# Latent layers: second attention's projections and rotation ahead of the gated linear attention's levels, one projection for two sets of values; context gates applied behind PSUM; key copies issued by GpSimd

## The chip, the cores and the metric

The kernel runs on one core of a Trainium2 chip. The metric is device time in microseconds (us) of one execution. The engines are named PE (TensorE, matmuls), DVE (VectorE), ACT (ScalarE), POOL (GpSimd) and SP (SyncE, which issues most of the DMAs); each has an instruction queue of its own, executed in order.

## The reference, cut to what matters

Two blocks are computed one after the other, in float32. The first (dilated attention with an mLSTM, cross attention, a mixture of 16 experts) is not touched. The second has two layers, in which a latent stream `x` (512 tokens, width 1024) and a context stream `ctx` (256 tokens) go through three mixers side by side: a neighbourhood attention (na, 6 heads of 64), a gated linear attention (GLA, 4 heads) and a grouped-query attention (GQA, 6 query and 2 key heads). The latent stream's two attentions also read the context's keys and values. One input projection feeds all three:

```python
(na_q, na_k, na_v, gl_q, gl_k, gl_v, gl_g, gl_lr, ga_q, ga_k, ga_v) = jnp.split(u @ w_in, IN_SPLITS, axis=-1)
# widths 384, 384, 384, 128, 128, 256, 256, 32, 384, 128, 128
...
o = jnp.concatenate([merge_heads(o_na), gla_output(o_gl, gla_norm_w, gl_g), merge_heads(o_ga)], axis=-1)
...
x = layer_norm(DEEPNORM_ALPHA * x + g1 * (o @ w_out[l]), ln1_g[l], ln1_b[l])
x = layer_norm(DEEPNORM_ALPHA * x + g2 * swiglu(modulate(x, sh2, sc2), w_ffn_in[l], w_ffn_out[l]), ln2_g[l], ln2_b[l])
if ctx_out:     # layer 0 only
    xc = layer_norm(DEEPNORM_ALPHA * xc + g1c * (oc @ w_out[l]), ln1_g[l], ln1_b[l])
    xc = layer_norm(DEEPNORM_ALPHA * xc + g2c * swiglu(modulate(xc, sh2c, sc2c), w_ffn_in[l], w_ffn_out[l]), ln2_g[l], ln2_b[l])
```

GQA's queries and keys are normed by head (rms) and rotated by an axial position table ahead of the scores. The gates g1, g2 (g1c, g2c) are one row of 1024 numbers for all tokens.

## The kernel before

**Products.** Every float32 operand is split into a high part (`w_h`, a cast by ACT, L350) and a low part (`w_l`, the rest, a subtraction by DVE, L351), and a product is three matmuls, high by high, high by low and low by high (L343). A weight chunk goes DMA (`raw`, L380) → optionally a multiplication by a row on POOL (L387) → the two splits → matmuls. A projection by tokens (`proj_tok`, matmuls named `pj`) goes over column blocks of up to 512, each into one PSUM bank per tile of 128 tokens (four for the latent stream, two for the context); with K = 1024 that is 8 × 3 × 4 = 96 matmuls per column block of the latent stream and 48 of the context. A projection by features (`pf`) takes 128 columns at a time.

**Order.** The framework orders each engine's instructions when the kernel is built: by the place in the program among those that its own timeline takes to be ready. So of two pieces of work that are both ready, the one written earlier goes first, and later work fills the gaps. Buffers and PSUM banks are given out in that order. Several places write the order out by hand, with Python generators that are advanced piece by piece.

**Stages.** Until about 480 us the first block runs up to its experts. From there to 1204 us the experts run in the background of the context stream's layer 0 (its second stream of weight chunks), to 1284 us the context's layer 1 (keys and values only). Then come latent layer 0 (1284 to 1978 us) and latent layer 1 (to the end).

**A layer** (`layer2`, L2149) runs `gla` first: the gate inputs (L1839), the gates themselves (L1848 to L1862), q and k, a projection of 512 columns for v and the output gate, transposed decayed keys (`gltp`, L1906), the chunk states (`gls`), eight levels `lv` that fill the attention matrix (L1943 to L2002: on POOL a difference `glD`, on ACT two exponentials for each direction and scaled copies `glqb`, on DVE products `glxk` and `glxq`, on PE the matmuls `glG`), and the output products (`glo`, L2013 and L2017). `finish` norms, gates and transposes its output (`otp`, L2035). Then `gqa` (L1700): a projection of 512 columns for q and k (L1719), one of 128 for v (L1721), through `between` the neighbourhood attention's 384 columns for its values (`na_v`, L1575), then for each tile of tokens the rotation on DVE and POOL, a transposition (`gtp`, L1783) and the splits. Between these, `woven` advances `na_kq` (L1585), which projects the neighbourhood attention's first pair of keys (K0) and queries (Q0) and later those of pairs 1 and 2. The scores (`sc`, L542 and L543) of the neighbourhood attention follow, with a bias that POOL loads (`na_bias`, L1621).

**Key copies.** Keys stand in two halves of the partitions; `dup_k` (L530) copies each half to the other with four DMAs from SP's queue, for GQA's keys (`gak`) and for each pair of neighbourhood keys (`nak`).

**Gates.** In the latent stream `out_proj` (L2076) multiplies the product by g1 on DVE (`gps`, L2086). In the context stream (`nt < 4`) the gate is multiplied into the weight chunks instead, by POOL, through `row=`: 8 chunks of `w_out` and 22 of `w_ffn_out`, each 128x1024 (L387). `ffn` (L2096) does that in both streams for g2.

## Time and profile before

| | us |
|---|---|
| median of 3 runs (lowest, highest) | 2701.52 (2699.83, 2702.96) |
| profiled execution: its time | 2709.36 |
| profiled execution: span of its trace | 2707.6 |
| PE busy in the span | 2515.4 |
| DVE, ACT, POOL busy | 1725.2, 1281.9, 418.7 |

The span is what the trace covers; 1.8 us of the profiled execution's time lie around it. Durations in the rows are those of this one execution. Matmuls are pipelined, and the duration of one overlaps the next: the cost of many in a row is the length of their stretch over their count, not the mean of one.

### The profile page before, as it was taken

Reading aid. Unit: us, or ns where it says so; the run is one execution under the profiler, and the core shown is the slowest. Engines: PE = TensorE matmul, PEld = TensorE weight load, DVE = VectorE, ACT = ScalarE, POOL = GpSimd, SP = SyncE. Lnnn points to the kernel's source line nnn. Section 1 sums busy time; section 2 is a strip of 40 time slices with the busy share of each in tenths; the row PEclk is TensorE's granted clock in tenths of the full one; section 3 lists DMA queues with packets and bytes.
Section 4 is the critical chain, followed back from the end, with each engine's and each line's share of the span. In section 5 each row is a group of like instructions: output and inputs, shape, how many; then the busy total and the mean of one; then the engine's idle time right before and its main releaser. Section 6 shows DMA issues by size and latency. Waiting matters only on the chain. (4 is left out here: it accounts for less than half of the span.)

```text
span 2707.6 us, 35926 instructions
## 1 busy us (share of the span) xinstructions
PE 2515.4 (93%) x13176; PEld 1963.8 (73%) x13176; DVE 1725.2 (64%) x3117; ACT 1281.9 (47%) x2389; POOL 418.7 (15%) x304
## 2 busy tenths in 40 slices
PE   8999899798889999988998999999989899999997
PEld 5547575676667888877786588888868666888886
DVE  3346646797687787778786665444567776644446
ACT  4344444576655555556656642222266574422221
POOL 1100000201022121022220023111141200411101
PEclk9999899899999999998999999999989999999999
DMA  7765357588777888767254123333323524233331
GB/s 276 208 203 160 117 192 244 159 268 282 250 241 234 268 276 276 252 222 220 81 156 137 69 87 122 96 94 94 104 86 96 146 82 133 71 101 93 94 93 63
DMA packets 355157, 436.54 MB, mean 161 GB/s; under 512 B 20384, under 2 KB 228128, under 8 KB 354976
## 3 DMA queue, kind: packets, MB, share of 16 engines
q1 hardware_dynamic: 350560, 416.90, 49.1%
q0 software_dynamic: 4416, 17.30, 1.8%
q8 instruction: 105, 1.72, 0.3%
q14 instruction: 76, 0.62, 0.1%
HBM read 387.21 MB, written 38.01 MB: 157 GB/s over the span
## 5 line engine op out<-in xcount | busy, mean ns | idle before, releaser
L351 DVE TENSOR_TENSOR w_l<-raw,w_h 128x1024 fp32r<-128x1024 f32 (+2 forms) x530 | 714.5, 1359 | 465.8 <-ACT w_h L350 456.6
L350 ACT CAST w_h<-raw 128x1024 fp32r<-128x1024 f32 (+2 forms) x530 | 527.5, 1007 | 855.6 <-PE pj L343 272.2
L343 PE MATMUL fab<-hTf_h,w_h 128*128 128x512 f32 (+1 forms) x1104 | 386.2, 351 | 4.1 <-ACT hTf_h L514 3.4
L343 PE MATMUL fab<-hTf_h,w_l 128*128 128x512 f32 (+1 forms) x1104 | 386.7, 351 | 0.5 <-DVE w_l L351 0.4
L343 PE MATMUL fab<-hTf_l,w_h 128*128 128x512 f32 (+1 forms) x1104 | 386.2, 350 | 0.2
L387 POOL TENSOR_TENSOR raw<-raw,g2b 128x1024 f32<-128x1024 f32 x66 | 172.3, 2617 | 708.5 <-DMA raw<-in_w_ffn_out 615.1
L343 PE MATMUL pj<-w_l,hT_h 128*128 128x512 f32 (+3 forms) x608 | 229.8, 379 | 14.1 <-DVE w_l L351 14.1
L343 PE MATMUL pj<-w_h,hT_h 128*128 128x512 f32 (+3 forms) x608 | 222.2, 378 | 14.9 <-ACT w_h L350 9.9
L343 PEld LDWEIGHTS fab<-hTf_h,w_h 128*128 128x128 f32 x1104 | 208.9, 190 | 37.2 <-ACT hTf_h L514 4.5
L343 PEld LDWEIGHTS fab<-hTf_h,w_l 128*128 128x128 f32 x1104 | 209.2, 190 | 32.8 <-DVE w_l L351 1.2
L343 PEld LDWEIGHTS fab<-hTf_l,w_h 128*128 128x128 f32 x1104 | 209.2, 190 | 32.2 <-DVE hTf_l L515 0.6
L343 PE MATMUL pj<-w_h,hT_l 128*128 128x512 f32 (+3 forms) x608 | 225.0, 372 | 0.0
L343 PE MATMUL pj<-w_h,wk_h 128*128 128x512 f32 x376 | 148.5, 401 | 7.9 <-DVE x L2107 4.9
L343 PEld LDWEIGHTS pj<-w_h,hT_h 128*128 128x128 f32 x608 | 118.6, 197 | 45.8 <-ACT w_h L350 13.4
L343 PEld LDWEIGHTS pj<-w_l,hT_h 128*128 128x128 f32 x608 | 120.5, 198 | 42.4 <-DVE w_l L351 18.3
L343 PE MATMUL pj<-w_l,wk_h 128*128 128x512 f32 x376 | 150.0, 400 | 1.1 <-DVE w_l L351 0.9
L343 PE MATMUL pj<-w_h,wk_l 128*128 128x512 f32 x376 | 147.3, 399 | 1.2 <-DVE wk_l L351 1.2
L343 PE MATMUL pf<-hT_h,w_h 128*128 128x512 f32 (+3 forms) x376 | 133.4, 356 | 10.2 <-DVE nak_l L351 3.1
L343 PEld LDWEIGHTS pj<-w_h,hT_l 128*128 128x128 f32 x608 | 120.3, 198 | 22.0 <-issue 5.2
L343 PE MATMUL pf<-hT_h,w_l 128*128 128x512 f32 (+3 forms) x376 | 131.2, 350 | 0.0
L343 PE MATMUL pf<-hT_l,w_h 128*128 128x512 f32 (+3 forms) x376 | 131.2, 350 | 0.0
L577 ACT COPY pT<-ptp 128x512 f32<-128x512 f32 (+3 forms) x184 | 88.5, 497 | 53.5 <-PE ptp L575 52.4
(598 smaller groups left out, 4840.7 us busy)
## 6 DMA issues: line engine op xcount, KB each, us to landing
raw<-in_w SPq DMA_DIRECT2D x192, 512.0 KB
raw<-in_w_ffn_in SPq DMA_DIRECT2D x132, 512.0 KB
raw<-in_w_ada SPq DMA_DIRECT2D x96, 512.0 KB
raw<-in_w_in SPq DMA_DIRECT2D x76, 512.0 KB
raw<-in_w_ffn_out SPq DMA_DIRECT2D x66, 512.0 KB
raw<-in_w_out SPq DMA_DIRECT2D x32, 512.0 KB
yd<-ysb SPq DMA_DIRECT2D x16, 512.0 KB
raw<-in_w_in SPq DMA_DIRECT2D x16, 384.0 KB
```

The source lines that it names most:

```text
L343: self.nc.tensor.matmul(out, lhsT=l, rhs=r, start=first and k == 0 and i == 0, stop=last and k == n - 1 and i == 2, **kw)
L350: nc.scalar.copy(out=hl.hi, in_=src)
L351: nc.vector.tensor_sub(out=hl.lo, in0=src, in1=f32(hl.hi))
L387: self.nc.gpsimd.tensor_tensor(out=raw, in0=raw, in1=row.unsqueeze(1).to_broadcast([P, kt, n]), op=OP.mult)
L577: nc.scalar.copy(out=pT()[:, slice(b0, b0 + bb), ts], in_=tp[:, :bb * P].rearrange("p (b t) -> p b t", t=P))
```

## The change

`w_in`'s columns are put in another order on the host, so that GQA's v (128 columns) and the neighbourhood attention's v (384) are neighbours and one projection of 512 columns makes both, in all four layers (latent and context). `gqa` becomes a generator with two stops: in the latent layers `gla` advances it, once behind its own q and k (GQA's q and k projection), once behind its v and gate projection (the V projection, the rotation, transpositions, splits and key copies), so that all of this stands ahead of GLA's levels in the program. The neighbourhood attention's K0 is started behind `gla`, no longer within the rotation. In the context layers the order stays. In `out_proj` and `ffn` of the context the gate is multiplied by DVE with the product's PSUM tile (`times`), no longer into the weights by POOL. In the latent layers `dup_k` issues from POOL's queue.

```diff
@@ -197,6 +197,9 @@
...
     A["w_out_2"] = np.concatenate([wo[:, :640], wo[:, 640:].reshape(2, 2, 3, 64, D).transpose(0, 2, 1, 3, 4).reshape(2, 384, D)], 1)
+    wi = A["w_in_2"]
+    A["w_in_2"] = np.concatenate([wi[:, :, :768], wi[:, :, 1152:], wi[:, :, 768:1152]], 2)
@@ -520,17 +523,17 @@
...
-    def stack_k(self, k, ps):
+    def stack_k(self, k, ps, eng=None):
...
             self.split(k[r, h], ps[r])
-        self.dup_k(k)
-    def dup_k(self, k):
+        self.dup_k(k, eng)
+    def dup_k(self, k, eng=None):
...
             for h in range(2):
-                self.nc.sync.dma_start(out=f32(t[64 - 64 * h:128 - 64 * h, h]), in_=f32(t[64 * h:64 * h + 64, h]))
+                (eng or self.nc.sync).dma_start(out=f32(t[64 - 64 * h:128 - 64 * h, h]), in_=f32(t[64 * h:64 * h + 64, h]))
@@ -1572,22 +1575,12 @@
...
-    def na_v(self, l, hT, T, W, pool):
-        vd = self.dr.tile([T, 384], F32, name=f"nav{l}{T}")
-        def ev(i, c0, n, ps):
-            v = pool.tile([P, 384], F32, name="nav", tag="nav", bufs=2)
-            self.copy(v, ps[:, :n])
-            self.nc.sync.dma_start(out=vd[i * P:(i + 1) * P, :], in_=v)
-        self.proj_tok(hT, T // P, W[:, 768:1152], ev)
-        return vd
...
         k = g["k"] = self.hl_tile(pool, [P, 2, T], "nak", f"nak{f % 2}")
-        yield from self.feat_pieces(hT, T, W[:, 384 + f * P:384 + (f + 1) * P], lambda ps: self.stack_k(k, ps[:, :T]))
+        yield from self.feat_pieces(hT, T, W[:, 384 + f * P:384 + (f + 1) * P], lambda ps: self.stack_k(k, ps[:, :T], nc.gpsimd if lat else None))
@@ -1697,7 +1690,7 @@
...
-    def gqa(self, l, hT, T, W, ctxd, full, d, keep, pool, between, woven):
+    def gqa(self, l, hT, T, W, ctxd, full, d, keep, pool, got):
@@ -1705,7 +1698,7 @@
...
         nh = nq + 2
-        c0 = 1952 if full else 2336
+        c0 = 1568 if full else 1952
@@ -1717,9 +1710,17 @@
...
         self.proj_tok(hT, nt, W[:, c0:c0 + nh * 64], ev)
+        yield
         v = keep.tile([P, nt, P], F32, name="gav")
-        self.proj_tok(hT, nt, W[:, 2464:2592], lambda i, c0, n, ps: self.copy(v[:, i, :], ps[:, :n]))
-        mid = between()
+        vd = self.dr.tile([T, 384], F32, name=f"nav{l}{T}")
+        def ev_v(i, _, n, ps):
+            self.copy(v[:, i, :], ps[:, :P])
+            t = pool.tile([P, 384], F32, name="nav", tag="nav", bufs=2)
+            self.copy(t, ps[:, P:n])
+            nc.sync.dma_start(out=vd[i * P:(i + 1) * P, :], in_=t)
+        self.proj_tok(hT, nt, W[:, 2080:2592], ev_v)
@@ -1775,8 +1776,6 @@
...
             ff = f.rearrange("p h d -> p (h d)")
-            for _ in range(2):
-                next(woven, None)
@@ -1787,7 +1786,7 @@
...
                 self.split(kS[r2, h, ts], tp[r2, (nb - 1) * P:nb * P])
-        self.dup_k(kS)
+        self.dup_k(kS, nc.gpsimd if lat else None)
@@ -1823,9 +1822,10 @@
...
             return units
-        return attend, mid
-    def gla(self, l, hT, T, W, ctxd, full, d, late, pool):
+        got.extend((attend, vd))
+        yield
+    def gla(self, l, hT, T, W, ctxd, full, d, late, pool, other):
@@ -1836,10 +1836,10 @@
...
         if lat and l:
-            lr_, *qk = self.in_halves(hT, T, [W[:, a:b] for a, b in ((1920, 1952), (1152, 1280), (1280, 1408))], lambda: self.mm("pf"))
+            lr_, *qk = self.in_halves(hT, T, [W[:, a:b] for a, b in ((1536, 1568), (768, 896), (896, 1024))], lambda: self.mm("pf"))
...
         else:
-            self.proj_feat(hT, T, W[:, 1920:1952], lambda f, m, ps: nc.scalar.copy(out=lr, in_=ps[:32, :T]))
+            self.proj_feat(hT, T, W[:, 1536:1568], lambda f, m, ps: nc.scalar.copy(out=lr, in_=ps[:32, :T]))
@@ -1872,7 +1872,8 @@
...
         else:
-            self.proj_feat(hT, T, W[:, 1152:1408] if full else W[:, 1280:1408], ev)
+            self.proj_feat(hT, T, W[:, 768:1024] if full else W[:, 896:1024], ev)
+        next(other, None)
@@ -1886,9 +1887,10 @@
...
                                                op0=OP.mult, op1=OP.mult)
-            self.proj_tok(hT, nt, W[:, 1408:1920], evv)
+            self.proj_tok(hT, nt, W[:, 1024:1536], evv)
         else:
-            self.proj_tok(hT, nt, W[:, 1408:1664], lambda i, c0, n, ps: self.copy(v[:, i, :], ps[:, :n]))
+            self.proj_tok(hT, nt, W[:, 1024:1280], lambda i, c0, n, ps: self.copy(v[:, i, :], ps[:, :n]))
+        next(other, None)
@@ -2065,6 +2067,11 @@
...
+    def times(self, ps, g, pool):
+        t = pool.tile([P, 512], F32, name="gps", tag="gps", bufs=1)
+        self.nc.vector.tensor_tensor(out=t, in0=ps, in1=g, op=OP.mult)
+        return t
@@ -2081,16 +2088,13 @@
...
             s = slice(c0, c0 + n)
-            if nt == 4:
-                t = pool.tile([P, 512], F32, name="gps", tag="gps", bufs=1)
-                nc.vector.tensor_tensor(out=t, in0=ps, in1=g1b[:, s], op=OP.mult)
-                ps = t
-            nc.vector.scalar_tensor_tensor(out=x[:, i, s], in0=x[:, i, s], scalar=ALPHA, in1=ps[:, :n], op0=OP.mult, op1=OP.add)
+            nc.vector.scalar_tensor_tensor(out=x[:, i, s], in0=x[:, i, s], scalar=ALPHA, in1=self.times(ps, g1b[:, s], pool),
+                                           op0=OP.mult, op1=OP.add)
...
         if nt < 4:
-            return self.proj_tok(oT, nt, W, lambda *a: self.call(ev(*a)), row=g1b)
+            return self.proj_tok(oT, nt, W, lambda *a: self.call(ev(*a)))
@@ -2104,6 +2108,8 @@
...
             s = slice(c0, c0 + n)
+            if nt < 4:
+                ps = self.times(ps, g2b[:, s], pool)
@@ -2133,7 +2139,8 @@
...
             if f0 < nf or nt < 4:
-                self.proj_tok(lambda k: gT[:, k, :], nt, rows, ev if f0 < nf else lambda *a: self.call(ev_last(*a)), kt=fg, row=g2b)
+                self.proj_tok(lambda k: gT[:, k, :], nt, rows, ev if f0 < nf else lambda *a: self.call(ev_last(*a)), kt=fg,
+                              row=g2b if nt == 4 else None)
@@ -2159,14 +2166,21 @@
...
             with tpool("gqp") as p2, tpool("gll") as p0:
+                got = []
+                second = self.gqa(l, hT, T, W, ctxd, full, d, keep, p2, got)
                 with tpool("glp") as p1:
-                    finish = self.gla(l, hT, T, W, ctxd, full, d, p0, p1)
+                    finish = self.gla(l, hT, T, W, ctxd, full, d, p0, p1, second if lat else iter(()))
...
                 begun = self.na_kq(0, l, hT, T, W, lat, full, p3, g0, d) if lat else iter(())
-                attend, vd = self.gqa(l, hT, T, W, ctxd, full, d, keep, p2, lambda: self.na_v(l, hT, T, W, p2), begun)
+                if lat:
+                    next(begun)
+                    next(begun)
+                for _ in second:
+                    pass
+                attend, vd = got
```

## Rows read from the trace of the kernel before

**Rows 1.** The page: busy time of the engines, and the chain that ended last.

```profile
PE 2515.4 (93%) x13176; PEld 1963.8 (73%) x13176; DVE 1725.2 (64%) x3117; ACT 1281.9 (47%) x2389; POOL 418.7 (15%) x304
...
PE 19%; DVE 1%; DMA 1%; ACT 0%; issue 0%; DVEq 0%
```

**Rows 2.** Windows: stretch, length, busy (count) per engine, granted PE clock, DMA share, GB/s.

```profile
820.00:1200.00 380.00, 362.32 (x2072) 311.97 (x2072) 293.39 (x308) 210.03 (x261) 66.66 (x29) 0.98 0.78 254
...
1284.00:1400.00 116.00, 116.00 (x788) 97.00 (x787) 86.40 (x168) 72.42 (x152) 27.72 (x30) 1.00 0.38 114
1400.00:1411.00 11.00, 5.50 (x30) 4.79 (x29) 10.69 (x28) 5.22 (x13) 3.14 (x4) 0.69 0.66 213
...
2118.00:2129.00 11.00, 5.37 (x28) 4.51 (x27) 10.65 (x29) 5.04 (x15) 3.14 (x4) 0.84 0.59 191
```

**Rows 3.** Windows of the projections `pj` alone, 512, 128 and 384 columns.

```profile
1294.03:1316.39 22.36, 22.36 (x96) 17.81 (x95) 0.41 (x1) 0.90 (x3) 1.00 0.28 87
1353.52:1355.79 2.27, 2.27 (x19) 2.20 (x19) 0.00 (x0) 0.00 (x0) 1.00 0.23 30
1379.76:1387.93 8.17, 8.17 (x46) 8.01 (x46) 0.00 (x0) 0.96 (x2) 1.00 0.10 33
```

**Rows 4.** Timeline, PE, first latent layer: start, duration, instruction, idle before.

```profile
1316.39 1.04 PE L1906 MATMUL gltp<-cpack,glt 128*128 128x128 f32 x8
...
1329.47 1.08 PE L1981 MATMUL glG<-glqb,glk 128*32 128x128 f32 x32
...
1370.43 0.70 PE L2013 MATMUL glo<-glSc,glqt 128*128 128x256 f32 x2
...
1378.94 1.00 PE L2017 MATMUL glo<-glv,glA 128*128 128x64 f32 x8
...
1406.60 0.58 PE L542 MATMUL sc<-nak_h,naq 128*128 128x256 f32 x1 [3.04 <-DVE glost L351]
```

**Rows 5.** Timeline, DVE, same layer.

```profile
1307.54 0.41 DVE L1962 TENSOR_TENSOR glxk<-glD,glk 128x256 f32<-128x256 f32 x1
...
1308.21 0.68 DVE L1902 TENSOR_TENSOR glt<-glt,glk 128x512 f32<-128x512 f32 x1
```

**Rows 6.** Timeline, ACT, same layer.

```profile
1353.42 0.40 ACT L1960 ACTIVATE glD<-glD 128x256 f32<-128x256 f32 x1
...
1363.22 2.51 ACT L1971 ACTIVATE glqb<-glxq,cpack 128x256 f32<-128x256 f32 x6 [0.51 <-DVE glxq L1963]
```

**Rows 7.** Timeline, SP's queue (SPq: the time an issue held it).

```profile
1419.95 4.27 SPq L533 DMA_DIRECT2D gak_h<-gak_h  x1
...
1427.66 0.94 SPq L533 DMA_DIRECT2D nak_h<-nak_h  x1
```

**Rows 8.** Chain of waits, second latent layer: start, duration, piece.

```profile
2148.92 10.19 DMA nak_l<-nak_l
```

**Rows 9.** The bias tile `nab`, loaded from POOL's queue.

```profile
DMA to landing us min/median/max: 3.8/5.9/8.2
```

**Rows 10.** Groups by line and form, 440 to 1210: busy, mean ns | idle before, releasers.

```profile
L351 DVE TENSOR_TENSOR w_l<-raw,w_h 128x1024 fp32r<-128x1024 f32 x283 | 377.4, 1352 | 126.7 <-ACT w_h L350 122.8 <-PE fab L343 2.7
...
L343 PE MATMUL h<-w_l,ehT_h 128*128 128x512 f32 x256 | 104.2, 407 | 8.5 <-DVE w_l L351 8.5
...
L387 POOL TENSOR_TENSOR raw<-raw,g2b 128x1024 f32<-128x1024 f32 x22 | 58.5, 2664 | 215.7 <-DMA raw<-in_w_ffn_out 156.1 <-DVE w_l L351 37.1 <-DVE wk_l L351 19.7
...
L343 PE MATMUL pj<-w_h,wk_h 128*128 128x512 f32 x88 | 34.8, 420 | 7.9 <-DVE x L2107 4.9 <-ACT w_h L350 2.7 <-ACT wk_h L350 0.2
...
L387 POOL TENSOR_TENSOR raw<-raw,g1b 128x1024 f32<-128x1024 f32 x8 | 20.0, 2509 | 51.8 <-DMA raw<-in_w_out 21.0 <-issue 15.6 <-DMA nak_h<-nak_h 15.2
```

**Rows 11.** Waits of ACT, 440 to 1210: total, times, longest.

```profile
ACT w_h L350 <- POOL raw L387: 53.6, 21, 6.2
```

**Rows 12.** The tile `w_l`, 480 to 1200: ns min/median/max, first and last start.

```profile
L351 DVE TENSOR_TENSOR w_l<-raw,w_h x292: 411/1222/3439, 480.7 to 1198.6; 128x1024 fp32r<-128x1024 f32 x141, 128x256 fp32r<-128x256 f32 x3, 128x768 fp32r<-128x768 f32 x2
```

**Rows 13.** The tile `gps`, whole run.

```profile
L2086 DVE TENSOR_TENSOR gps<-pj,g1b x16: 672/679/693, 1568.2 to 2318.9; 128x512 f32<-128x512 f32 x16
```

## The prediction

> **What bounds the kernel now.** I began with the page's busy shares and its chain of waits. TensorE (PE) is busy in 2515.4 of 2707.6 us, and the chain that ended last runs mostly through PE's matmuls [rows 1]. So a change pays if it takes matmul time away, or one of the stretches in which PE stands still. The table by stretch says where these are [rows 2]. The context layer, with the experts beside it, leaves PE idle for 380.00 − 362.32 = 17.7 us in 820–1200. In the first latent layer's projections (1284–1400) PE is busy for all 116.00 us at a granted clock of 1.00, the upper of its two levels (2.4 GHz). Behind them lies a hole of 11 us with 5.50 us busy, in which the mean granted clock is 0.69, between the upper level and the lower one (1.2 GHz). The second latent layer repeats it at 2118–2129 (5.37 us). So idle time per latent layer is 5.5 us, in which the rotated queries and keys and the first neighbourhood scores are waited for: PE then begins the scores after 3.04 us idle, released by a DVE subtract [rows 4].
>
> **Merged V projection.** It removes 96 matmuls with 128 columns and 96 with 384 in each latent layer and adds 96 with 512. From the three stretches of projection matmuls alone [rows 3], one costs 2.27/19 = 0.1195 us, 8.17/46 = 0.1776 us and 22.36/96 = 0.233 us. Per layer 96 × (0.1195 + 0.1776 − 0.233) = 6.2 us. PE has no idle time there [rows 2], so this is on the path: −12.3 us for both. In each context layer it is 48 × 0.064 = 3.1 us of PE time, but PE there has gaps and experts to fill them; between 0 and −6.2 for both, I take −2.5. Copies out of PSUM move the same 512 columns as before.
>
> **The new order of the latent layers.** Nothing is added; what changes is what stands first when PE may choose. In the old order the gated linear attention (GLA) stands ahead of the grouped-query attention (GQA): its levels break into the GQA projection whenever one is ready, and the projection fills the rest. In the trace of before, work with a later place in the program waits, ready or not: the second decayed key tile was written by DVE at 1308.21 + 0.68 [rows 5], but its transposition began at 1316.39, with the end of the value/gate projection's 96 matmuls [rows 4]. In the new order all three 512-column projections stand ahead of the levels, so the levels lose their filling. What is left as filling is the neighbourhood attention's first key and query pair.
>
> The time that GLA then takes, counted from the end of the last projection: from the transposition to the first level 1329.47 − 1316.39 = 13.1 us, eight levels 1370.43 − 1329.47 = 41.0, output products to 1379.94 = 9.5 [rows 4], together 63.5 us as it ran with PE shared. With PE free a level costs at least what ACT does for it: 2.51 us for six scaled copies and four exponentials of 0.40, 4.1 us [rows 6], 7 × 4.1 = 28.7, and 13.1 + 28.7 + 9.5 = 51.3. One level's factors are ready beforehand, as they were at 1307.54, 9 us before the projection's end [rows 5], which leaves 51.3 − 4.1 = 47.2 us.
>
> The PE work for this time: of the 116.00 us, the tail of the GLA's q/k projection until 1294.03 is 10.0, the four projections are 22.4 + 22.4 + 11.5 + 17.1, and the stretch 1387.93 to 1400 (neighbourhood K and Q of the first pair) is 12.1. GLA's own matmuls are the rest, 116.0 − 95.5 = 20.5. With 48 × 0.233 = 11.2 for K0 and Q0 and, as an estimate from the 5.50 us busy in the hole, 4 for the transpositions, that is 36 us; with K1 (24 × 0.233 = 5.6) 41.6, with Q1 too 47. K1's buffer lies over that of the rotation and comes free early; Q1's lies over GLA's temporary tiles and doesn't. I take 41.6, and 47.2 − 41.6 = 5.6 us idle, against 5.5 now. So the hole is only moved: 0 per layer, +1 in all for what the rotation takes from DVE and POOL ahead of the levels. Bounds per layer: −5.5 (no hole) and 63.5 − 36 − 5.5 = +22. I take the low middle, because one level's factors and the rotation can be done during the third projection, when PE needs the other engines only for weights (ACT 72.42 and DVE 86.40 of 116 us busy [rows 2]).
>
> **Key copies by POOL.** Each latent layer's 16 copies (GQA keys and three neighbourhood pairs, four each) go from SP's queue to POOL's. On SP the copy of the GQA keys at 1419.95 held the queue for 4.27 us, and the neighbourhood copy behind it went out at 1427.66 [rows 7]. In the second layer a copy lay on the chain for 10.19 us [rows 8]. POOL's own loads of the bias took 3.8 to 8.2 us from issue to landing [rows 9]. So a copy lands between 10.2 − 3.8 = 6.4 us earlier and, where POOL has other work or waits, up to 8.2 us later. PE has other heads' products to do while a copy is under way, so I take −1 for each layer, near nothing: −2, bounds −6.4 and +16 (8.2 in each layer). The new wait: a copy on POOL waits for the split keys, and behind it on POOL stand the levels' subtractions and the bias loads. ACT waits for those, PE for ACT. SP's queue, freed, only gets its neighbourhood value loads out earlier.
>
> **Context gates from PSUM.** It removes 30 multiplications on POOL: 22 with g2b (mean 2664 ns) and 8 with g1b, some 78 us of POOL time [rows 10], and the waits of ACT on them, 53.6 us in 21 waits, the longest 6.2 [rows 11]. PE's own waits that hang on this are smaller. The two groups of [rows 10] that name weights, the experts' products behind the low part (8.5) and the feed-forward products behind the high part (2.7), make 11.2 us. It adds 28 DVE multiplications of 128x512 at 679 ns [rows 13], 19.0 us, each between a bank's last matmul and its release. PE already waits 4.9 us for the add in that place [rows 10]; with two operations in place of one that doubles, +4.9. Against that DVE gets time back. Its low-part subtractions have a mean of 1352 ns but a median of 1222, with one of 3439 [rows 10, 12]; if all of the excess is POOL's, 283 × 0.13 = 37 us of DVE time goes. The rule behind it is told by the Trainium skill ("SBUF — State Buffer", section "SBUF: two separate sides"): the pair of ports that VectorE and GpSimd share is a lock, held for a whole instruction. By that rule DVE gains 37 − 19 = 18 us of free time here; without it, DVE has 19 us more to do. The sum takes neither: −10 of the 11.2, +5 for the release, −5. Bounds: −17.7 (all of PE's idle time in 820–1200) and +19.
>
> **Sum.** The profiled run took 2709.36 us (2707.6 span, 1.8 around it), 7.8 above the median of the runs. −12.3 − 2.5 + 1 − 2 − 5 = −20.8, so 2688.6 for such a run, and 2701.5 − 20.8 = **2681 us** at the median. The likeliest case's own range, with its unknown terms halfway to their bounds, is 2666 to 2696.
>
> **Rivals.** A, slower: the levels starve. They keep the 63.5 us and PE has 41.6 to do, so 21.9 − 5.5 = 16.4 us more idle time per layer: 2681 − 1 + 33 = 2713, and with 36 us of work 2723. It decides as soon as PE's idle time between the last projection's end and the neighbourhood scores passes 5.5 + (12.3 + 2.5 + 2 + 5)/2 = 16.4 us per layer. For it: ACT's 28.7 us of levels are a chain, POOL's copies may stand in it, the levels lose 22 us of filling. Against it: one projection's time to prepare. 0.24.
> B, no change: the added 19 us of DVE work all lie between PE and its banks: 2681 + 5 + 19 − 5 = 2700. For it: DVE is the busiest engine beside PE there (293.39 of 380 us [rows 2]); against it, POOL's work goes. 0.13.
> C, faster still: no hole (−11 − 1), and the context gains 17.7 in place of 5: 2681 − 12 − 13 = 2656. 0.13.
> D, copies late: with POOL as issuer one copy of each layer is waited for to its full 8.2 us: 2681 + 2 + 16 = 2699. The Trainium skill (same page and section) warns of this: descriptors of a DMA issued from GpSimd can't be written while VectorE holds the shared ports. [...] 0.05.
>
> **How the numbers follow.** Likeliest case 0.45. To leave out no more than 2 in 10, the range reaches from C's 2656 to A's upper end: 2655 to 2722. A change within 0.2% (5.4 us) can't be told from none. Faster: likeliest and C, and a little of B and D, 0.60. Same: most of B and D, 0.16. Slower: A, 0.24.
>
> **What would show it.** Right: in each latent layer a projection of 96 matmuls of 512 columns in place of the two; 5 to 6 us of PE idle time between the third projection and the scores; first level directly behind the third projection, K1's matmuls before the last output product; in the context 30 fewer multiplications of weights, ACT's waits for POOL gone, the mean of the low-part subtraction near 1222 ns; copies issued from POOL that nobody waits over 2 us for. Wrong: more than 16 us idle between the projections and the scores (A); PE waiting in the context for the new multiplications by over 10 us (B); PE waiting on a key copy (D).

## The result and the profile after

The changed kernel takes 2721.82 us (median of 6 runs, 2713.09 to 2727.10), the kernel before 2700.68 (6 runs, 2694.79 to 2704.42): a ratio of 1.0076, interval 1.0053 to 1.0100, so 21 us slower where 20.8 us faster was forecast. The profiled execution after took 2727.1 us with a span of 2725.2, 17.6 us over the span before.

Where the time went is seen first by cutting both traces at the same instructions (starts on PE: the first gate matmul `glz`, the experts' last product `yps`, the first neighbourhood score, the first feed-forward matmul `fab`):

| stretch, us | before | after |
|---|---|---|
| start to the context layer 0's gates | 485.6 | 487.6 |
| context layer 0 beside the experts | 713.4 | 692.5 |
| combine stage and context layer 1 | 87.9 | 96.3 |
| latent layer 0: gates to first score, then to feed-forward | 119.7 + 190.8 | 140.9 + 185.9 |
| latent layer 0: feed-forward | 405.9 | 407.2 |
| latent layer 1: gates to first score, then to feed-forward | 120.5 + 194.9 | 140.7 + 185.6 |
| latent layer 1: feed-forward to the end | 388.9 | 388.5 |

The context gives 12.5 us, the two latent layers take 16.3 and 10.9. The profiled execution before was a long one (2709.4 us, the median 2700.7): in e4 below, whose context is that of before, the context takes 792.0 us and not 801.3, so most of the 12.5 may belong to that one execution. In a latent layer the first score comes 20 to 21 us later, and 5 to 9 us of that are made good by then finished work.

The page of the changed kernel, busy times (beside [rows 1]):

```profile
PE 2503.8 (92%) x12888; PEld 1939.3 (71%) x12888; DVE 1716.6 (63%) x3129; ACT 1282.2 (47%) x2373; POOL 348.1 (13%) x306
```

PE does 11.6 us less and POOL 71 us less, and yet the span grows. The stretches of the first latent layer (columns as in [rows 2]) tell why: two projections, the third (V), and the hole behind it.

```profile
1274.00:1330.00 56.00, 56.00 (x241) 44.12 (x240) 39.35 (x64) 33.97 (x57) 11.26 (x14) 1.00 0.34 103
1330.00:1353.00 23.00, 23.00 (x101) 18.70 (x100) 7.32 (x11) 6.05 (x12) 0.47 (x1) 1.00 0.36 105
1353.00:1418.00 65.00, 45.27 (x393) 34.94 (x392) 53.24 (x126) 41.84 (x101) 20.54 (x28) 0.82 0.28 85
```

While PE makes the V projection, DVE is busy for 7.32 of 23 us and ACT for 6.05. Then PE is idle for 65.00 − 45.27 = 19.7 us of the next 65, at a mean granted clock of 0.82, and DVE is the busiest engine with 53.24. In [rows 2] the same work left 5.5 us of idle time. PE's timeline in the hole (beside [rows 4]):

```profile
1353.66 1.04 PE L1782 MATMUL gtp<-cpack,gsq 128*128 128x128 f32 x8
1354.70 0.70 PE L1930 MATMUL gls<-glv,glkt 128*128 128x256 f32 x2
1355.33 1.08 PE L1983 MATMUL glG<-glqb,glk 128*32 128x128 f32 x32
...
1360.98 1.08 PE L1983 MATMUL glG<-glqb,glxk 128*32 128x128 f32 x16 [4.57 <-DVE glqb L1975]
1362.64 1.08 PE L1983 MATMUL glG<-glqb,glxk 128*32 128x128 f32 x16 [0.57 <-DVE glqb L1975]
1365.90 1.09 PE L1782 MATMUL gtp<-cpack,gsq 128*128 128x128 f32 x4 [2.18 <-DVE gsq L1775]
1370.85 1.94 PE L1983 MATMUL glG<-glqb,glxk 128*32 128x128 f32 x32 [3.86 <-DVE glqb L1975]
...
1398.53 3.68 PE L1983 MATMUL glG<-glqb,glxk 128*64 128x256 f32 x16 [3.33 <-ACT glqb L1973]
1402.14 1.22 PE L2015 MATMUL glo<-glSc,glqt 128*128 128x256 f32 x2
...
1415.68 1.94 PE L2037 MATMUL otp<-cpack,glos 128*128 128x128 f32 x8 [5.21 <-DVE glos L2032]
1417.28 0.57 PE L545 MATMUL sc<-nak_h,naq 128*128 128x256 f32 x1
```

The first level starts behind the V projection and is not followed by the second for over 5 us, since DVE's part of its factors isn't ready. The eight levels take 1402.14 − 1355.33 = 46.8 us, against 41.0 before [rows 4]. Of the 19.7 us of idle time 12.3 lie ahead of levels (4.57 + 0.57 + 3.86 + 3.33, the first 9.0 of them for DVE's scaled copies `glqb`), 2.2 ahead of a rotated tile's transposition and 5.2 ahead of that of the finished output (`otp`). Why no second level was ready stands in POOL's and ACT's timelines:

```profile
1329.43 1.05 POOL L1959 TENSOR_TENSOR glD<-gla_b 128x512 f32<-128x512 f32 x1 [10.24 <-PE gltp L1908]
1358.38 1.46 POOL L1764 TENSOR_TENSOR gu<-gsq,tsq 128x192 f32<-128x192 f32 x2 [27.91 <-DVE gsq L1749]
```

```profile
1346.54 1.05 ACT L353 CAST w_h<-raw 128x1024 fp32r<-128x1024 f32 x1 [4.48 <-PE pj L346]
...
1356.04 2.51 ACT L1973 ACTIVATE glqb<-glxq,cpack 128x256 f32<-128x256 f32 x6 [0.84 <-PE glG L1983]
```

A level's difference tile (`glD`) waited for a buffer that the decayed keys gave up only with their transposition, which stood behind PE's matmuls; the rotation waited 27.91 us, two rotated tiles holding both buffers until PE transposed them at 1353.66 (they were written before 1321). ACT's queue holds casts that wait for PE. So DVE, ACT and POOL stood still for PE, and then PE for them. How much shorter the hole would be without these waits is not shown: in e15 and e16 below the rotation's is gone, but another of the same kind takes its place.

In the context the gates did more than forecast. Groups by line, 440 to 1210 (beside [rows 10]):

```profile
L354 DVE TENSOR_TENSOR w_l<-raw,w_h 128x1024 fp32r<-128x1024 f32 x287 | 350.6, 1236 | 115.9 <-ACT w_h L353 114.9 <-PE pf L346 0.2
L346 PE MATMUL h<-w_l,ehT_h 128*128 128x512 f32 x256 | 103.8, 406 | 0.3
L346 PE MATMUL pj<-w_h,wk_h 128*128 128x512 f32 x88 | 33.6, 395 | 0.7 <-ACT w_h L353 0.5 <-DVE gps L2072 0.2
```

The low-part subtraction fell from 1352 to 1236 ns, the experts' 8.5 us of waits for it to 0.3, and the 4.9 us behind the adds are gone, though each of them now has a multiplication ahead of it. In e2 below, the gates alone, that mean is 1234, and in e3, which keeps POOL's multiplications, 1341.

### The profile page after: what moved, and what is told of

The parts are those of the page before. It is cut to its first block, busy times and chain, and to the rows that moved or that the text cites. A ratio compares the mean times of both kernels' runs of the same rounds, so it can differ in the third digit from the quotient of the medians.

```text
span 2725.2 us, 35255 instructions
## 1 busy us (share of the span) xinstructions
PE 2503.8 (92%) x12888; PEld 1939.3 (71%) x12888; DVE 1716.6 (63%) x3129; ACT 1282.2 (47%) x2373; POOL 348.1 (13%) x306
## 3 DMA queue, kind: packets, MB, share of 16 engines
q1 hardware_dynamic: 343648, 412.70, 47.2%
## 4 chain that ended last, share of the span: by engine, by line
PE 56%; DVE 9%; DMA 6%; ACT 5%; issue 2%; SPq 1%; POOL 1%; DVEq 0%; ACTq 0%; POOLq 0%
PE fab L346 22%; PE pj L346 18%; PE h L346 3%; PE oat L638 3%; PE yps L346 3%; DVE w_l L354 3%; PE pf L346 2%; DMA raw<-in_w 2%; PE ptp L578 1%; ACT w_h L353 1%; SPq L1650 1%; DMA navc<-nav 1%; PE sc L545 1%; ACT glqb L1973 1%; PE tp L503 1%
## 5 line engine op out<-in xcount | busy, mean ns | idle before, releaser
L354 DVE TENSOR_TENSOR w_l<-raw,w_h 128x1024 fp32r<-128x1024 f32 (+1 forms) x514 | 671.6, 1316 | 472.6 <-ACT w_h L353 457.8
L353 ACT CAST w_h<-raw 128x1024 fp32r<-128x1024 f32 (+1 forms) x514 | 524.9, 1032 | 871.1 <-PE pj L346 295.0
L346 PE MATMUL pj<-w_l,hT_h 128*128 128x512 f32 (+2 forms) x512 | 204.1, 399 | 8.3 <-DVE w_l L354 8.3
L346 PE MATMUL pj<-w_h,hT_h 128*128 128x512 f32 (+2 forms) x512 | 196.9, 399 | 14.4 <-ACT w_h L353 11.2
L346 PE MATMUL pj<-w_h,hT_l 128*128 128x512 f32 (+2 forms) x512 | 200.5, 394 | 0.0
L390 POOL TENSOR_TENSOR raw<-raw,g2b 128x1024 f32<-128x1024 f32 x44 | 112.8, 2572 | 495.9 <-DMA raw<-in_w_ffn_out 484.2
L346 PEld LDWEIGHTS pj<-w_h,hT_h 128*128 128x128 f32 x512 | 97.5, 192 | 45.6 <-ACT w_h L353 12.9
L346 PEld LDWEIGHTS pj<-w_l,hT_h 128*128 128x128 f32 x512 | 98.4, 192 | 39.8 <-DVE w_l L354 12.5
L346 PEld LDWEIGHTS pj<-w_h,hT_l 128*128 128x128 f32 x512 | 98.5, 192 | 25.0 <-issue 4.2
```

The source lines that it names most:

```text
L346: self.nc.tensor.matmul(out, lhsT=l, rhs=r, start=first and k == 0 and i == 0, stop=last and k == n - 1 and i == 2, **kw)
L353: nc.scalar.copy(out=hl.hi, in_=src)
L354: nc.vector.tensor_sub(out=hl.lo, in0=src, in1=f32(hl.hi))
L390: self.nc.gpsimd.tensor_tensor(out=raw, in0=raw, in1=row.unsqueeze(1).to_broadcast([P, kt, n]), op=OP.mult)
```

## The experiments

Theory: the new order puts PE's three projections in one piece and leaves the other engines' work for afterwards. Rivals: the key copies on POOL's queue; the evacuation of the merged projection; something in the context. All times are medians beside runs of the kernel before with medians of 2698.5 to 2702.7; ratios are to those.

**Each part by itself.** e1 is the changed kernel with the old order:

```diff
-                second = self.gqa(l, hT, T, W, ctxd, full, d, keep, p2, got)
...
-                    finish = self.gla(l, hT, T, W, ctxd, full, d, p0, p1, second if lat else iter(()))
+                    finish = self.gla(l, hT, T, W, ctxd, full, d, p0, p1, iter(()))
...
-                    next(begun)
-                    next(begun)
-                for _ in second:
+                for _ in self.gqa(l, hT, T, W, ctxd, full, d, keep, p2, got, begun):
                     pass
```

> The changed kernel with the old order of the latent layers put back: GLA whole, then GQA with the first neighbourhood pair woven into its rotation. The merged V projection, the context gates and the key copies by POOL stay. Theory (the order starves the levels): from the start of the gates to the first neighbourhood scores the two traces differ by +21.2 and +20.2 us, of which 4.9 and 9.3 come back by the feed-forward part, and the merge is in that with -6.2 each; so the order costs about 22 and 17 us, and this kernel takes 2722 - 39 = 2683 us, PE idle under 8 us in each hole. Rival 1 (the key copies on POOL's queue hold up the levels): still over 2710. Rival 2 (the merged projection's evacuation, two buffers whose DMA is waited for): also over 2710, with the idle time at the V projection's end.

Measured 2701.91 us, ratio 1.000 (0.998 to 1.002). The order costs 2721.8 − 2701.9 = 20 us, not 39: its latent layers take 315.4 and 313.3 us from the gates to the feed-forward part, 11.4 and 13.0 less than after. Rivals 1 and 2 fall as the cause by themselves, as copies and merge are still in e1. But a kernel with gates, merge and copies that is no faster than before says that something in these costs what the gates give.

e2 is the kernel before with the gates alone (the change's hunks in `out_proj` and `ffn`), e3 with the merge alone (the columns and the V projection), e4 with the copies alone (`dup_k` on POOL):

```diff
-            return self.proj_tok(oT, nt, W, lambda *a: self.call(ev(*a)), row=g1b)
+            return self.proj_tok(oT, nt, W, lambda *a: self.call(ev(*a)))
```
```diff
-        self.proj_tok(hT, nt, W[:, 2464:2592], lambda i, c0, n, ps: self.copy(v[:, i, :], ps[:, :n]))
-        mid = between()
+        self.proj_tok(hT, nt, W[:, 2080:2592], ev_v)
```
```diff
-        self.dup_k(kS)
+        self.dup_k(kS, nc.gpsimd if lat else None)
```

> The kernel before with only the context gates taken from PSUM by DVE. My forecast for this part was -5 (between -17.7 and +19). From the two traces the context layer 0 with the experts is 21 us shorter and the following combine stage 8 us longer; if all of this is the gates' doing: 2701 - 12 = 2689 us. Rival (the gain in the context comes from the merged projections or from another order of the work): within 3 us of 2701.

> The kernel before with only the columns put in the other order and one V projection of 512 columns, in its old place. By the sum of the matmuls -12.3 in the latent layers and 0 to -6 in the context: 2686 to 2689 us. Rival (the narrow projections fill gaps that the levels leave, so that their time was not on the path): 2695 to 2701 with more idle time ahead of the scores.

> The kernel before with only the latent layers' key copies issued from POOL's queue. Forecast -2 (between -6 and +16): 2699 us. Rival 1 (copies wait behind POOL's work or hold up the levels' subtractions and the bias loads): 2710 us and more, PE idle with a key copy or a bias tile as the releaser.

e2 took 2671.45 us, ratio 0.990 (0.987 to 0.992): 28.5 us faster. Its stretch from the context's first feed-forward matmul to the experts' last product:

```profile
813.90:1161.40 347.50, 344.51 (x2040) 302.09 (x2039) 271.35 (x319) 204.52 (x254) 6.12 (x6) 1.00 0.83 271
```

and the same stretch of the kernel before:

```profile
818.80:1199.40 380.60, 363.30 (x2074) 312.66 (x2074) 293.99 (x308) 209.99 (x261) 67.86 (x29) 0.98 0.79 255
```

It is 33 us shorter (29 against the same stretch in e4, 375.9 us); 17.3 − 3.0 = 14.3 of them were idle time of PE, and the rest is busy time: 34 matmuls had moved ahead of it, and the mean granted clock is 1.00 in place of 0.98. POOL's multiplications held up both ACT [rows 11] and DVE; which of the two gave how much no run separates.

e3 took 2716.29 us, ratio 1.0063 (1.0044 to 1.0083): the merge alone costs 16 us, where 12 to 15 less was forecast. The last stretch before the scores in its first latent layer, and PE's waits there:

```profile
1356.00:1400.00 44.00, 28.11 (x139) 21.55 (x137) 33.37 (x78) 16.80 (x37) 9.97 (x16) 0.78 0.31 100
```
```profile
1381.01 1.11 PE L1791 MATMUL gtp<-cpack,gsq 128*128 128x128 f32 x4 [9.36 <-DVE gsq L1782]
1385.36 0.90 PE L1791 MATMUL gtp<-cpack,gsq 128*128 128x128 f32 x3 [3.23 <-DVE gsq L1782]
```

PE is idle for 15.9 us ahead of the scores, 12.6 of them for the rotation (the two lines), three times the 5.5 of [rows 2]. And the levels come slower. Three of them in e3:

```profile
1339.17 1.08 PE L1989 MATMUL glG<-glqb,glxk 128*32 128x128 f32 x32
1345.51 1.08 PE L1989 MATMUL glG<-glqb,glxk 128*32 128x128 f32 x32
1351.84 1.08 PE L1989 MATMUL glG<-glqb,glxk 128*32 128x128 f32 x32
```

and in the kernel before, beside the 128-column projection (a level is one row of x32 or two of x16):

```profile
1347.38 1.08 PE L1981 MATMUL glG<-glqb,glxk 128*32 128x128 f32 x32
1351.45 0.64 PE L1981 MATMUL glG<-glqb,glxk 128*32 128x128 f32 x16
1352.95 0.64 PE L1981 MATMUL glG<-glqb,glxk 128*32 128x128 f32 x16
1355.79 0.65 PE L1981 MATMUL glG<-glqb,glxk 128*32 128x128 f32 x16
```

6.3 us from level to level against 4.1 to 4.3. PE's order is fixed when the kernel is built, and in it 22 projection matmuls stand between two of these levels of e3 and 26 between two of the kernel before: 22 × 0.233 = 5.1 us with 512 columns, 26 × 0.1195 = 3.1 with 128 [rows 3]. In e3 the level's last scaled copy was done 1.0 to 3.1 us before PE came to it, in the kernel before 0.2 and 0.5 us (the levels at 1351.45 and 1355.79). The narrow matmuls let the levels through sooner, and the 384-column ones were still there to cover the output products and the rotation.

e4 took 2697.46 us, ratio 0.9992 (0.9975 to 1.0009): nothing that can be told from none.

**Gates and copies together**, and the context's cost of the merge. e9 is e2 with e4's edit; e8 is e1 with

```diff
+        if not lat:
+            self.pump(2)
         self.proj_tok(hT, nt, W[:, 2080:2592], ev_v)
+        if not lat:
+            self.pump(2)
```

> The kernel before with the two parts that did not cost anything by themselves: context gates behind PSUM (-28.5 alone) and the key copies by POOL (-2.5 alone, not clear of nothing). If they add: 2669 us. If the copies had only moved noise: 2671 to 2672.

> The kernel of e1 (old order, merged V, context gates behind PSUM, copies by POOL) with the background advanced by four more chunks' worth around the context layers' V projection, as the four weight chunks that the merge took away had advanced it. In e1 94 of the experts' 1152 matmuls are left when the context's feed-forward part ends, in the kernel with the gates alone 24, and the experts then run alone from 1141 to 1175 us. Theory (the merge takes steps from the background, which then runs alone): about 24 matmuls are left again, the experts' end comes some 13 us earlier and the combine stage is back to 88 to 90 us: 2702 - 13 - 5 = 2684 us. Rival (the merged projection itself costs the context its gain, through its evacuation or the width of its chunks): within 4 us of 2702.

e9 took 2668.81 us, ratio 0.988 (0.986 to 0.991), as the parts add, and is with e18 below the fastest kernel here that leaves nothing out: 53 us faster than the change. e8 took 2686.33 us, ratio 0.993 (0.991 to 0.996), 15.6 less than e1, with 24 expert matmuls left as expected. The end of the experts in e1, from the end of the context's feed-forward part:

```profile
1141.00:1175.00 34.00, 29.27 (x126) 22.71 (x124) 30.18 (x56) 23.02 (x33) 0.00 (x0) 0.90 0.58 186
```

and in e9:

```profile
1149.00:1158.00 9.00, 7.88 (x38) 5.97 (x37) 8.47 (x22) 3.98 (x6) 0.00 (x0) 1.00 0.35 101
```

The background is advanced with each weight chunk of the foreground. The merge has four chunks where there were eight, so the context goes through sooner and leaves the experts 34 us alone instead of 9. By the traces this costs time only beside the new gates: in e3, with POOL's multiplications, 72 expert matmuls are left, and yet its context takes 789.3 us against 792.0 in e4. So the merge costs 16 us by itself and 2701.9 − 2668.8 = 33 us beside gates and copies.

e17 and e18 are e9 with the merge in the context's layer 0 alone and in its layer 1 alone:

```diff
+        if not lat and full:
+            self.proj_tok(hT, nt, W[:, 2080:2592], ev_v)
+        else:
...
+            mid = between()
```

> The kernel of e9 (gates and copies, 2669 us) with the merged V projection in the context's layer 0 alone, beside the experts. If the lost background steps there are most of the 21 us: +13, 2682 us, and 94 expert matmuls left when the feed-forward part ends. If the cost lies in layer 1: within 3 of 2669.

> The kernel of e9 with the merged V projection in the context's layer 1 alone, beside the combine stage. From the combine stage's length with the merge (94 us after the experts' end, 90 without): +4 to +8, 2673 to 2677 us. If layer 1 doesn't count: within 3 of 2669.

e17 took 2678.10 us (ratio 0.993, 0.991 to 0.995), +9.3, with 94 expert matmuls left; e18 2668.14 (0.990, 0.987 to 0.992), nothing. So layer 0 is the larger part. With both layers merged the trace of e1 has 17 us more than e9 in the context, and what the two do together beyond the 9 stays open.

**The latent order taken apart.** e5 moves the V projection of the changed kernel behind the levels (and in the context behind GQA's keys), the rotation stays ahead; e10 adds e8's edit; e14 is the changed kernel with V in two pieces; e13 is e14 with the pieces behind the levels in the latent layers.

```diff
-        self.proj_tok(hT, nt, W[:, 2080:2592], ev_v)
...
         self.dup_k(kS, nc.gpsimd if lat else None)
+        yield
...
+        self.proj_tok(hT, nt, W[:, 2080:2592], ev_v)
```
```diff
-        self.proj_tok(hT, nt, W[:, 2080:2592], ev_v)
+        self.proj_tok(hT, nt, W[:, 2080:2208], lambda i, c0, n, ps: self.copy(v[:, i, :], ps[:, :n]))
...
+        self.proj_tok(hT, nt, W[:, 2208:2592], ev_v)
```

> The changed kernel with the V projection taken out of the part that stands ahead of GLA's levels and put behind them; GQA's q and k projection, the rotation, the transpositions and the copies stay ahead. Theory (the levels take their time from ACT and DVE, and what counts is how much PE work is left beside them and which work then waits): 96 matmuls, 22 us, are beside the levels again, and the rotation is done by then; PE's 20 us idle in each layer fall to under 8 and 2722 - 24 = 2698 us. Rival 1 (the levels are held up by the rotation standing ahead of them on DVE and POOL): no better than 2715. Rival 2 (the copies on POOL): no better than 2715, with the levels' subtractions behind a copy on POOL.

> The kernel of e5 with the same four more background steps as in e8 around the context layers' V projection. If both theories hold: 2698 - 18 = 2680 us; if only the one on the context, 2722 - 18 = 2704; if only the one on the latent order, 2698.

> The changed kernel with V projected as before in two pieces (128 and 384 columns), in the new order. Theory: in the latent layers the two pieces stand ahead of the hole, where PE is busy anyway, so +6.2 each; in the context the four chunks more bring the background's steps back, -15 to -18: 2722 + 12 - 17 = 2717 us. Rival (the merge costs in the latent layers in any order): 2695 or less.

> As e5, but with V in two pieces, in the latent layers behind GLA's levels and in the context where it was. Theory: the latent layers take e5's 315 us from the gates to the feed-forward part or a little less, as the narrow pieces give the levels more to run beside (e9: 312 and 310), and the context is that of e9: 2669 + 7 = 2676 us, 2669 at best. If the rotation ahead is worth having by itself, less than 2665; if e5's 12 us idle time is the rotation's doing, still 2676 and more.

e5 took 2708.26 us, ratio 1.0015 (0.9999 to 1.0030). Its latent layers take 315.0 + 314.1 us from the gates to the feed-forward part against 326.8 + 326.3 after: the 24 us that were expected. Its combine stage, however, is 108.2 us long against 96.3, which the expectation had left out. e10 took 2704.98 (1.0010, 0.9992 to 1.0027), a miss: e5 had only 24 expert matmuls left, so there was nothing to give back.

e14 took 2703.51 us, ratio 1.0013 (0.9998 to 1.0027), between the two expectations. Its latent layers take 332.0 + 329.9 us, so in the new order the merge saves 5.2 and 3.6 a layer, close to the 6.2 of matmul time, and its context takes 25 us less than after. Against e9 (312.4 + 309.5), which differs from it by the order alone (and by where the columns lie in `w_in`), the order costs 19.6 and 20.4 us a layer, by the medians 34.7 for both. In the first layer 13.5 of the 19.6 are idle time; the other 6.1 are busy time of PE for the same matmuls, 1720 in e14 and 1719 in e9, at a mean granted clock of 0.94 and 0.97:

```profile
1248.90:1580.90 332.00, 296.79 (x1720) 224.91 (x1720) 221.96 (x534) 193.04 (x438) 38.95 (x54) 0.94 0.36 107
1248.80:1561.20 312.40, 290.66 (x1719) 222.33 (x1719) 223.35 (x534) 190.86 (x438) 42.22 (x54) 0.97 0.38 114
```

The two stretches of e14 that answer to those of after:

```profile
1302.00:1331.00 29.00, 29.00 (x201) 28.79 (x199) 12.67 (x22) 8.40 (x16) 1.04 (x1) 1.00 0.45 126
1331.00:1394.00 63.00, 45.34 (x393) 34.96 (x393) 50.79 (x119) 42.75 (x101) 20.71 (x28) 0.83 0.34 97
```

The longer projection (29 against 23 us) bought next to nothing: the hole behind it is nearly as long.

e13 took 2698.56 us, ratio 0.9987 (0.9973 to 1.0001), 22 above its expectation. V's pieces stand late in PE's order, and most of them (138 of 192 matmuls) are not worked on in the hole but behind it:

```profile
1305.00:1358.00 53.00, 38.21 (x351) 27.97 (x350) 42.12 (x93) 32.85 (x85) 18.21 (x25) 0.72 0.19 55
1358.00:1400.00 42.00, 42.00 (x253) 39.31 (x253) 21.33 (x52) 17.95 (x32) 2.08 (x4) 0.99 0.59 172
```

**What the hole is made of.** e11 and e12 leave four levels out, of the changed kernel and of e9; e15 gives the rotated tiles four buffers, e16 takes the rotation's products away, both from the changed kernel:

```diff
-        for lv in range(8):
+        for lv in ((0, 5, 6, 7) if lat else range(8)):
```
```diff
-        sq = lambda: pool.tile([P, nh, 64], F32, name="gsq", tag="gsq", bufs=2)
+        sq = lambda: pool.tile([P, nh, 64], F32, name="gsq", tag="gsq", bufs=4 if lat else 2)
```

> The changed kernel with four of GLA's eight levels (1 to 4) left out in the latent layers, so that part of the attention matrix is missing. Theory (in the new order the levels' work on ACT, DVE and POOL sets the time of the hole): PE's 20 us idle time ahead of the scores falls to some 4, beside 4 x 1.08 us of matmuls per layer: about -20 for each layer, 2722 - 40 = 2682 us. Rival (the hole comes from the rotation or the copies, and the levels only stand in it): only PE's part goes, -9 in both, 2713 us.

> The kernel of e9 (old order, separate V projections, gates and copies) with the same four levels left out. Theory (in the old order PE is what sets the time, the levels run beside its projections): only the matmuls go, 4.3 us a layer, and some of the 5.5 idle: 2669 - 9 to - 15 = 2654 to 2660 us. Rival (the levels set the time in either order): -16 to -20 a layer, 2633 us.

> The changed kernel with four buffers in place of two for the rotated tiles in the latent layers, so that all four tiles can be rotated while PE works through the projections. If the rotation of tiles 2 and 3 in the hole is part of its cause: DVE's 2.2 us for each tile and POOL's 2 us leave it, -5 for each layer, 2712 us. If the hole is made of levels and splits alone: 2719 to 2722 us.

> The changed kernel without the rotation's products in the latent layers (queries and keys are normed and transposed without position or norm weights): DVE loses 0.8 us a tile, POOL all of its part. The transpositions and the splits stay. If the rotation holds the levels up on DVE and POOL: -6 a layer or more, 2710 us and less. If what holds the hole open is the levels with the transposed tiles' splits: within 4 us of 2722.

e11 took 2697.00 us (ratio 0.999, 0.998 to 1.001), e12 2651.75 (0.982, 0.979 to 0.984): 12.4 us a layer off in the new order, 8.5 in the old. That is less of a difference than the theory asked for. The hole of e11 is 51 us long with 12.9 idle, in place of 65 with 19.7:

```profile
1348.00:1399.00 51.00, 38.12 (x268) 30.08 (x267) 40.26 (x99) 27.05 (x61) 10.48 (x21) 0.83 0.34 104
```

So a level is worth 14/4 = 3.5 us of the hole, and half the levels do not close it. And the old order isn't free of the levels either: there PE and the chain through the other engines end nearly together. e15 took 2717.00 us (ratio 1.007, 1.005 to 1.009), −4.8 where −10 or nothing was expected, and e16 2712.06 (1.007, 1.004 to 1.009), −9.7 where −12 or nothing was. The change itself has 1.005 to 1.010, so neither is told from it. Neither shortens the hole by much: 64.4 and 63.1 us against 65.2 in the changed kernel, from the V projection's end to the first score. The hole of e16:

```profile
1345.18:1408.25 63.07, 43.91 (x395) 34.05 (x394) 50.83 (x119) 41.81 (x100) 15.63 (x20) 0.83 0.32 94
```

With the rotation's products gone DVE still has 51 us to do in it, and PE waits 12.1 us for DVE's scaled copies of the levels, as in the changed kernel (12.3 for those of DVE and ACT). So the rotation by itself isn't what holds the levels up. But the two runs do not take the waiting for PE away. In e15 all four tiles are rotated by 1322, and POOL then waits for the first key copy, whose keys PE has still to transpose, with the next level's difference tiles behind it in POOL's queue (e16: 33.64 us):

```profile
1356.15 0.59 POOL L536 DMA_DIRECT2D gak_h<-gak_h  x1 [32.22 <-ACT gak_h L353]
1356.88 2.45 POOL L1959 TENSOR_TENSOR glD<-gla_b 128x512 f32<-128x512 f32 x2
```

So rival 1 comes back there: the new order with the key copies on SP's queue was not run. In the changed kernel itself these copies wait less than 2 us in all (1379 to 1383). What fills the hole besides (the splits of the transposed tiles, the states, the levels' own products) was not taken apart either.

## Why the prediction was wrong

- **The new order.** The mechanism was there as rival A, with its point of decision at 16.4 us of idle time; 19.7 and 20.2 were measured. The step that failed is the one that chose the low end: a level was priced at ACT's 4.1 us [rows 6], seven of them at 28.7, and the chain from the last projection at 47.2. Measured were 46.8 us for the eight levels and 65.2 for the chain, and what PE waits for in it is mostly DVE, which is busy for 53.24 of 65 us. How much of this each wait makes stays open, as e15 and e16 only put one wait in another's place. The reason given, "one level's factors and the rotation can be done during the third projection, when PE needs the other engines only for weights", held for the first level and for two of the four rotated tiles. For the rest the other engines had time (7.32 and 6.05 of 23 us busy) but no work they could start: it needed PE's transpositions, which stand behind the ready projection by the same rule that the prediction had read from [rows 4, 5]. It was applied to the levels and not to the transpositions. The order costs 20 us a layer beside two V pieces (e14 and e9) and 11.4 and 13.0 beside the merged one, where 0 was put; 6 to 7 us of each are not idle time but longer matmuls, which the prediction did not count.
- **The merge.** This is the term that was furthest off: −14.8 with the context, against +16.4 by itself (e3) and +33.1 beside gates and copies. −6.2 a layer was right as matmul time, and nearly right in the new order (−5.2 and −3.6, after against e14). In the old order it costs 3.0 and 3.8 (e1 against e9). The step that failed is "PE has no idle time there [rows 2], so this is on the path": PE was full to the last us, but with matmuls that kept company to a chain of equal length. Taking them out made the chain show, and the wide ones held it up: the first score comes 9 us later in e1 than in e9 (130.0 and 128.4 us from the gates, against 120.6 and 119.3), and 5 to 6 us come back behind it. In e3, whose latent layers differ from those of e1 by the copies alone, nothing comes back there (319.6 and 320.4 us a layer against 315.4 and 313.3); why is open.
- **The merge in the context.** −2.5 was put; e17 shows +9.3 for layer 0, and by the traces both layers cost 17 beside the new gates (e1 against e9), while e3 has −2.7 against e4. The step failed because it counted PE time only; the chunks also drive the background, and e8, which gives these steps back, gains 15.6.
- **The gates.** −5 was put, with −17.7 as the lower end; −28.5 was measured (e2). The sign and the releasers were right ([rows 10, 11] against the lines of after). The end was taken from PE's idle time in 820 to 1200 alone; the gain lies in that stretch, but part of it was busy time of PE. The +5 for the longer release didn't come: PE waits 0.2 us for the multiplications. Rival B falls. By the rule of the Trainium skill ("SBUF — State Buffer", section "SBUF: two separate sides"), DVE would get back what POOL's instructions locked; the trace agrees, with 1352 to 1236 ns and 26.8 us less in that one group of subtractions. In the trace of before, the 46 of them that overlap an instruction of POOL take 2.03 us on average, the other 237 1.22.
- **The copies.** −2 was put, −2.5 measured (e4), which the interval doesn't tell from nothing. Rival D isn't seen: the copies of the low-part neighbourhood keys landed after 3.5 to 8.2 us, and the scores waited for them 1.5 us in all in the changed kernel. The Trainium skill's warning there (same page and section) is for the time in which VectorE runs an instruction in its two-port mode; whether one ran while these copies were issued no run here shows. With the merged V the copies may be worth more than by themselves (e3 and e1, above).
- **The sum.** From 2700.7: gates −28.5 (e2), copies −2.6 (e9), merge +33.1 (e1), order +19.9 (after), together 2722.6 (the runs of before differ a little between the comparisons). The forecast had −5, −2, −14.8 and +1. That the time came near rival A's upper end is chance: A had the order at 33 and the rest at −22, where the order took 20 and the rest took 2, as the merge's loss ate the gates' gain.

## What to carry to other kernels

A full PE isn't proof that its matmuls are on the path: ask which chain they run beside, and what is uncovered when they go. Ask of work put ahead of a chain what it needs of the engine that it waits on: here the transpositions of the work moved forward stood behind the projections moved with them. The step of a chain through several engines is not the busy time of one of them: 4.1 us were taken from ACT, and 46.8/8 = 5.9 were measured. Where steps of one loop drive another piece of work (a background, a pump), fewer steps are a change of its own, and have to be counted like an instruction.

## What the runs showed of the hardware

In these traces the granted clock is lower in and just behind stretches with idle time of PE. In the V projection, with PE busy throughout, it was 1.00 (the upper level, 2.4 GHz). In the hole its mean was 0.82, between this and the lower one (1.2 GHz). From 1417.2 to 1420.0 it was 0.50, the lower level, and the first scores behind the hole start 0.21 to 0.22 us apart (timeline of PE, the changed kernel):

```profile
1417.64 0.41 PE L546 MATMUL sc<-nak_l,naq 128*128 128x256 f32 x1
1417.86 0.41 PE L545 MATMUL sc<-nakc_h,naq 128*128 128x256 f32 x1
```

In e11, whose PE had 8.6 us of `pf` matmuls in one piece shortly ahead of them, the same scores start 0.12 us apart, at 1.00:

```profile
1398.50 0.29 PE L546 MATMUL sc<-nak_l,naq 128*128 128x256 f32 x1
1398.62 0.28 PE L545 MATMUL sc<-nakc_h,naq 128*128 128x256 f32 x1
```

So a hole costs once more in the work that follows it: in the changed kernel some 20 scores until 1421.5 start 0.09 us further apart, an estimated 1.8 us. The kernel before pays this behind its own hole too (0.50 from 1406.6 to 1410.0), so it is no part of the difference; the 6.1 us of longer matmuls between e14 and e9 are.
